# Expert pairs of a mixture-of-experts trunk: the selector transposes go ahead of the token gathering, in another PSUM bank, and ScalarE takes every second eviction

## Chip, cores and metric

One Trainium2 chip, one core. The metric is the device time of one execution in microseconds (us), median of several runs. Engines are named as in the profile: PE (TensorE matmul), PEld (its weight loads), DVE (VectorE), ACT (ScalarE), POOL (GpSimd), SP (SyncE, which issues nearly all transfers).

## The reference

Two layers over 256 tokens of width 1024. Each layer is an attention sublayer ("mixing") and a mixture of experts; the change touches the experts only. In float32:

```python
g_val, g_idx = lax.top_k(g_prob, 1)                  # one of 4 groups per token
e_val, e_loc = lax.top_k(e_prob, TOP_K)              # 2 of its 8 experts
gate = g_val * e_val / jnp.sum(e_val, axis=-1, keepdims=True)
...
def run_block(args):
    e, idx, g = args
    xb = xt[idx]
    hb = jax.nn.silu(xb @ w1[e]) * (xb @ w3[e])       # 1024 -> 512
    return (hb @ w2[e]) * g[:, None].astype(x.dtype)  # 512 -> 1024
...
y = jnp.zeros_like(xt).at[tok_buf].add(y_buf.reshape(-1, d))
```

There are 32 experts per layer, with three weight matrices of 2 MB each.

## The kernel before

**Slots and selectors.** Each expert has room for 64 tokens (C = 64). A selector matrix says which token goes to which place: `placed(q)` builds `Dm[q]` for four experts on VectorE, and `gated(i)` multiplies the part of pair i with the gate values into `Dg`. Experts run in pairs: pair i is experts 2i and 2i + 1, and there are n = 16 pairs.

**The loop over pairs** (L1410 to L1434) is unrolled, and PE takes its instructions in the order written there (a manual schedule for PE); the other engines' orders come from the framework's planner, and tiles of one name in a pool share one buffer. For pair i PE runs: `up(i, 0)`, the two up projections of the first expert (L1359, 16 matmuls, 32 records in the profile, into bank `ph`); `y_part(i - 1, 0)` and `y_part(i - 1, 1)`, the down projections of the pair before (L1384, into banks `py` and `px`); `glu(i, 0)`, four transposes into bank `T` (L1200), from which ScalarE (L1202) and VectorE (L1203, L1204) make `gT`; `up(i, 1)`; `combine(i - 1)` (L1395), which adds the pair before to the four accumulators `acc`; on odd i `gather(q)`, which picks the tokens of the next two pairs with 32 short matmuls (L1302) in four blocks of two column groups, banks `px`, `py`, `px`, `py`, each block evicted by two VectorE instructions to `xg` (L1308); `glu(i, 1)`, again into `T`; and `scatter(i + 1)`: two transposes of `Dg` (L1338), also into bank `T`, from which VectorE takes `DT` (L1341) and `gate` (L1342). Only then comes `up(i + 1, 0)`. On i = 3 a residual is added by eight matmuls (L1284).

**Start and end.** `start_up()` routes the tokens, runs `gather(0)`, the projections of pair 0, `scatter(0)` and `glu(0, 1)`. The last pairs (L1435 to L1445) and the two loops' surroundings are as they were.

**Weights** stream from HBM through a ring of slots: `ring.free(...)` after the last reader of a slot lets SP issue the next transfer of a fixed list. The list follows the order of use: the first expert of a pair, the down weights of the pair before, the second expert. Blocks of 1024 KB hold half a matrix (L241); the last experts' down weights come as 512 KB blocks (L275). After the last expert of layer 0 the list goes on with the attention weights of layer 1.

Of the kernel before, what the change touches and what calls it, by code (L numbers as in the profile page):

```python
# [9 lines left out]
F32 = mybir.dt.float32  # L10
I32 = mybir.dt.int32
AF = mybir.ActivationFunctionType
OP = mybir.AluOpType
# [5 lines left out]
C = 64  # L19
# [138 lines left out]
def program(tc, I, out):  # L158
    nc = tc.nc
# [7 lines left out]
    def pool_(**kw):  # L167
        return tc.tile_pool(reuse_waits="tile", **kw)
# [202 lines left out]
    def warm(ps, n):  # L371

        for _ in range(n):
            nc.tensor.matmul(ps, ones, ones, start=True, stop=True)
# [734 lines left out]
    def experts(l, lg, logits, late, c2, acc, routed, two_parts):  # L1109
        nonlocal h  # L1110
        p1 = c2.enter_context(pool_(name=f"moe{l}", bufs=1))
        wkp = c2.enter_context(pool_(name=f"wk{l}", bufs=1, space=PS, side="right"))

        def start_up():
# [5 lines left out]
            steps, pos, OH, pair, vals = routing(lg, p1, wkp)  # L1120
            Dm[0] = p1.tile([128, 2, 4 * C], F32R, name="Dm")
            gathers = gather(0)
            two = [steps(t) for t in range(2)]
            for ahead in two:
# [46 lines left out]
            glu(0, 0, hs)  # L1171
            ph = next(up)
            scatter(0, gated(0))
            glu(0, 1, evacuated(ph))

# [14 lines left out]
        def evacuated(hps):  # L1190

            hs = p1.tile([128, 4, 128], F32, name="hs")
            nc.scalar.activation(hs, hps.rearrange("q (p j) -> q j p", j=4), AF.Copy)  # L1193
            return hs
# [63 lines left out]
        st, Dm, xg, gTs = {}, {}, {}, {}  # L1258
# [29 lines left out]
        def placed(q, *ts):  # L1288

            n = len(ts)  # L1290
            at = slice(ts[0], ts[0] + n)
            pv = pos[:, at, 4 * q:4 * q + 4, None].to_broadcast([128, n, 4, C])
            nc.vector.tensor_tensor(Dm[q][:, at].rearrange("p t (e s) -> p t e s", e=4),
                                    io[:, None, None, :].to_broadcast([128, n, 4, C]), pv, op=OP.is_equal)

        def gather(q):

            xg[q] = flex.tile([128, 8, 4 * C], F32, name="xg", tag="H")

            def product(px, k, t):  # L1300
                for i, x in enumerate(two_parts):
                    nc.tensor.matmul(px[:, k % 2], x[:, t, k], Dm[q][:, t], start=k % 2 == t == i == 0,  # L1302
                                     stop=k % 2 == t == i == 1, skip_group_check=True)

            def out(px, k0):
                for k in range(k0, k0 + 2):
                    g, b = ln[:, k:k + 1], ln[:, 8 + k:9 + k]
                    st["last"] = nc.vector.tensor_scalar(xg[q][:, k], px[:, k - k0], g, b, op0=OP.mult, op1=OP.add)  # L1308

            if q == 0:  # L1310
                px = [wkp.tile([128, 2, 4 * C], F32, name=name) for name in ("px", "py")]
                for t in range(2):
                    for k in range(4):
                        product(px[k // 2], k, t)
                        if t and k % 2:
                            out(px[k // 2], k - 1)
                    yield
            for k0 in range(0 if q else 4, 8, 2):
                px = wkp.tile([128, 2, 4 * C], F32, name="py" if k0 % 4 else "px")
                for k in range(k0, k0 + 2):  # L1320
                    for t in range(2):
                        product(px, k, t)
                out(px, k0)
            yield

        def gated(i):

            Dg = p1.tile([128, 2, 2, C], F32, name="Dg")
            D4 = Dm[i // 2].bitcast(F32).rearrange("p t (e s) -> p t e s", e=4)[:, :, 2 * (i % 2):2 * (i % 2) + 2]
            gv = G[:, :, 2 * i:2 * i + 2, None].to_broadcast([128, 2, 2, C])  # L1330
            nc.vector.tensor_tensor(Dg, D4, gv, op=OP.mult)
            return Dg

        def scatter(i, Dg):

            pd = wkp.tile([128, 2, 128], F32, name="T")
            for t in range(2):
                nc.tensor.transpose(pd[:, t], Dg[:, t].rearrange("p e s -> p (e s)"), ident)  # L1338
            DT = p1.tile([128, 2, 128], F32R, name="DT", bufs=2)
            gate = p1.tile([128, 1], F32, name="gate", bufs=2)  # L1340
            nc.vector.tensor_scalar(DT, pd, 0.0, None, op0=OP.is_gt)  # L1341
            nc.vector.tensor_reduce(gate, pd.rearrange("p t s -> p (t s)"), axis=AX.X, op=OP.add)  # L1342
            st[i] = dict(DT=DT, gate=gate)
# [22 lines left out]
        def glu(i, e, hs):  # L1366
            gT = p1.tile([128, 4, C], F32, name=f"gT{e}", tag=("Dg", "Dm")[e] if i == n - 1 else f"gT{e}")
            act_pair(hs, gT)
            gTs[i, e] = gT

        def y_part(i, a, fill=None, bank=None):

            ys = [out_parts[:, j, a] for j in range(2)]
            st[i]["ys", a] = ys
            cols = i >= n - 2
            W = [[ring[(l, "w2", 2 * i + e, half)].rearrange("p (j d) -> p j d", j=4 if cols else 2) for half in range(2)]
                 for e in range(2)]
            py = wkp.tile([128, 512], F32, name=bank or ("px" if a else "py"))
            for j in range(4):
                if fill and j == 2:  # L1380
                    fill()
                for e in range(2):
                    w = W[e][a][:, j] if cols else W[e][j // 2][:, j % 2, 512 * a:512 * a + 512]
                    nc.tensor.matmul(py[C * e:C * e + C], gTs[i, e][:, j], w, start=j == 0, stop=j == 3)  # L1384
            gate = st[i]["gate"]
            nc.scalar.activation(ys[0], py, AF.Copy, scale=gate)  # L1386
            nc.vector.scalar_tensor_tensor(ys[1], py, gate, ys[0].bitcast(F32), op0=OP.mult, op1=OP.subtract)  # L1387
            if a:
                ring.free(*[(l, "w2", 2 * i + e, half) for half in range(2) for e in range(2)])

        def combine(i, *parts):

            for t, a in parts:
                for j, y in enumerate(st[i]["ys", a]):
                    nc.tensor.matmul(acc[t][a], st[i]["DT"][:, t], y, start=False, stop=i == n - 1 and j == 1,  # L1395
                                     skip_group_check=True)
                if i == n - 1:
                    nc.vector.bn_stats(sts[t][:, a], acc[t][a])
# [6 lines left out]
        def up(i, e):  # L1405
            *_, ph = up_proj(i, e)
            return evacuated(ph)

        with tc.manual_schedule(engines={mybir.EngineType.PE}):
            for i in range(n - 1):  # L1410
                if i:
                    hs = up(i, 0)
                    for a in range(2):
                        y_part(i - 1, a)
                    glu(i, 0, hs)
                    hs = up(i, 1)
                if i % 2:
                    q = (i + 1) // 2
                    Dm[q] = p1.tile([128, 2, 4 * C], F32R, name="Dm")
                    placed(q, 0, 1)  # L1420
                if i:
                    combine(i - 1, *every)
                if i == 2:
                    residual = residual_ffn()
                    next(residual)
                if i == 3:
                    next(residual)
                if i % 2:
                    for _ in gather(q):
                        pass  # L1430
                Dg = gated(i + 1)
                if i:
                    glu(i, 1, hs)
                scatter(i + 1, Dg)  # L1434
            hs = up(n - 1, 0)  # L1435
            *_, ph = up_proj(n - 1, 1, bank="py")
            glu(n - 1, 0, hs)
            hs = evacuated(ph)
            for i in (n - 2, n - 1):
                first, second = ("px", "py") if i == n - 2 else ("py", "px")  # L1440
                y_part(i, 0, bank=first)
                if i == n - 2:
                    glu(n - 1, 1, hs)
                y_part(i, 1, lambda: combine(i, (0, 0), (1, 0)), bank=second)
                combine(i, (0, 1), (1, 1))  # L1445
            if l < L - 1:
                warm(wkp.tile([128, 128], F32, name="py"), 16)
# [27 lines left out]
    for l in range(L):  # L1475
        experts(l, *mixing(l))
# [48 lines left out]
```

## Time and profile before

| | us |
|---|---|
| median of 3 runs | 1476.15 (1475.31 to 1477.61) |
| profiled execution, its own time | 1479.88 |
| span of its profile | 1478.2 |
| PE busy | 1377.2 (93%) |
| DVE busy | 617.6 (42%) |
| ACT busy | 408.7 (28%) |
| q1, SP's transfers, share of 16 DMA engines | 84.6% |

Times in rows are us from the start of the span; a mean of one instruction is in ns. Busy PE includes matmuls that wait inside the array, so its share is not a share of peak.

### The profile page before, as it was taken

How to read it: one execution, taken by the hardware profiler on the slowest of the kernel's cores; microseconds unless marked ns; L12 is line 12 of the kernel's file. 1: busy time of each engine (PE TensorE's matmuls, PEld its weight loads, DVE VectorE, ACT ScalarE, POOL GpSimd, SP SyncE). 2: the span in 40 equal slices, each digit the busy share in tenths (PEclk: the TensorE clock that was granted, in tenths of full speed). 3: DMA queues.
4: the chain of work that ended last, by engine and by line, in shares of the span. 5: the costliest groups of instructions: out<-in, count | busy, mean ns of one | idle time of the engine just before them, and what ended most of it. 6: DMA issues, size and time to landing. Idle time of an engine off the chain costs nothing. (4 is left out here: it accounts for less than half of the span.)

```text
span 1478.2 us, 20321 instructions
## 1 busy us (share of the span) xinstructions
PE 1377.2 (93%) x8018; PEld 844.1 (57%) x8020; DVE 617.6 (42%) x1491; ACT 408.7 (28%) x858; POOL 88.8 (6%) x71
## 2 busy tenths in 40 slices
PE   8999999799999999999989999997999999999996
PEld 8999998433434434434389999983434434434432
DVE  6767777522212212212167776875212212212214
ACT  5566454211111111111145664541111010111111
POOL 2000030130000000000020000301300000000001
PEclk9999999799999999999999999999999999999998
DMA  9633788599999999999973438887999999999994
GB/s 349 207 115 129 251 319 298 190 326 417 419 419 420 419 420 420 418 420 418 383 250 114 116 128 282 322 295 251 374 419 419 419 420 419 421 420 419 419 408 152
DMA packets 114836, 488.74 MB, mean 331 GB/s; under 512 B 8624, under 2 KB 20400, under 8 KB 75440
## 3 DMA queue, kind: packets, MB, share of 16 engines
q1 hardware_dynamic: 114016, 486.26, 84.6%
q8 instruction: 65, 1.06, 0.3%
q10 hardware_dynamic: 720, 1.12, 0.2%
q14 instruction: 35, 0.29, 0.1%
HBM read 486.30 MB, written 1.05 MB: 330 GB/s over the span
## 5 line engine op out<-in xcount | busy, mean ns | idle before, releaser
L1359 PE MATMUL ph<-wslot,xg 128*64 128x512 f32 x1920 | 427.4, 597 | 0.0
L1359 PEld LDWEIGHTS ph<-wslot,xg 128*64 128x64 f32 x1920 | 132.8, 137 | 249.8 <-issue 246.6
L473 DVE TENSOR_TENSOR split<-wslot,split 128x512 fp32r<-128x512 f32 (+1 forms) x272 | 191.4, 715 | 95.2 <-ACT split L472 62.2
L472 ACT ACTIVATE split<-wslot 128x512 fp32r<-128x512 f32 (+2 forms) x276 | 168.8, 616 | 139.9 <-PE mm L504 119.6
L502 PE MATMUL mm<-hThi,split 128*128 128x256 f32 x704 | 202.3, 287 | 0.0
L504 PE MATMUL mm<-hThi,split 128*128 128x256 f32 x704 | 197.6, 281 | 0.3
L503 PE MATMUL mm<-hTlo,split 128*128 128x256 f32 x704 | 196.7, 279 | 0.0
L1193 ACT ACTIVATE hs<-ph 128x512 f32<-128x512 f32 x60 | 35.9, 598 | 452.8 <-PE ph L1359 439.2
L1387 DVE SCALAR_TENSOR_TENSOR ys<-py,gate,ys 128x512 fp32r<-128x512 f32 x32 | 24.0, 751 | 294.2 <-ACT ys L1386 294.2
L502 PEld LDWEIGHTS mm<-hThi,split 128*128 128x128 f32 x704 | 132.5, 188 | 3.7 <-ACT split L472 1.3
L504 PEld LDWEIGHTS mm<-hThi,split 128*128 128x128 f32 x704 | 132.3, 188 | 1.6 <-DVE split L473 1.5
L503 PEld LDWEIGHTS mm<-hTlo,split 128*128 128x128 f32 x704 | 132.5, 188 | 0.5 <-issue 0.5
L1384 PE MATMUL py<-wslot,gT 128*64 128x512 f32 x512 | 115.9, 593 | 0.0
L1384 PE MATMUL px<-wslot,gT 128*64 128x512 f32 x512 | 115.8, 593 | 0.0
L1203 DVE SCALAR_TENSOR_TENSOR th<-th,T 128x256 f32<-128x256 f32 x64 | 26.6, 416 | 166.3 <-ACT th L1202 166.3
L1308 DVE TENSOR_SCALAR xg<-px,cp 128x256 f32<-128x256 f32 x64 | 31.9, 540 | 133.9 <-PE px L1302 133.9
L1384 PEld LDWEIGHTS px<-wslot,gT 128*64 128x64 f32 x512 | 36.4, 137 | 71.9 <-issue 71.2
L1384 PEld LDWEIGHTS py<-wslot,gT 128*64 128x64 f32 x512 | 36.3, 137 | 71.4 <-issue 68.6
L1395 PE MATMUL acc<-ys,DT 128*128 128x512 f32 x256 | 70.5, 412 | 4.3 <-ACT ys L1386 3.2
L1395 PEld LDWEIGHTS acc<-ys,DT 128*128 128x128 f32 x256 | 45.3, 188 | 43.2 <-issue 26.0
L1202 ACT ACTIVATE th<-T 128x256 f32<-128x256 f32 x64 | 24.6, 384 | 146.3 <-PE T L1200 146.1
L1387 DVE SCALAR_TENSOR_TENSOR ys<-px,gate,ys 128x512 fp32r<-128x512 f32 x32 | 24.0, 751 | 85.3 <-ACT ys L1386 85.3
(311 smaller groups left out, 1755.9 us busy)
## 6 DMA issues: line engine op xcount, KB each, us to landing
wslot<-in_expert_w_dram SPq DMA_DIRECT2D x304, 1024.0 KB, 19.9
wslot<-in_expert_w_dram SPq DMA_DIRECT2D x160, 512.0 KB, 8.6
wslot<-in_w_gate_dram SPq DMA_DIRECT2D x16, 2048.0 KB, 9.9
wslot<-in_w_in_dram SPq DMA_DIRECT2D x6, 2048.0 KB, 14.9
wslot<-in_w_branch_dram SPq DMA_DIRECT2D x8, 1024.0 KB, 6.3
wslot<-in_w_out_dram SPq DMA_DIRECT2D x4, 2048.0 KB, 16.3
wslot<-in_w_in_dram SPq DMA_DIRECT2D x4, 1024.0 KB, 14.7
wslot<-in_w_in_dram SPq DMA_DIRECT2D x4, 832.0 KB, 10.3
```

Of the source, the lines that this page charges most:

```text
L472: nc.scalar.activation(hi, w, AF.Copy)
L473: engine.tensor_tensor(lo, w, hi.bitcast(F32), op=OP.subtract)
L502: nc.tensor.matmul(ps, st[0], mv[0], start=start, stop=False)
L503: nc.tensor.matmul(ps, st[0], mv[1], start=False, stop=False)
L504: nc.tensor.matmul(ps, st[1], mv[0], start=False, stop=stop)
L1193: nc.scalar.activation(hs, hps.rearrange("q (p j) -> q j p", j=4), AF.Copy)
L1203: nc.vector.scalar_tensor_tensor(th, th, 1.0, ps[:, :, 0:C], op0=OP.add, op1=OP.mult)
L1308: st["last"] = nc.vector.tensor_scalar(xg[q][:, k], px[:, k - k0], g, b, op0=OP.mult, op1=OP.add)
L1359: nc.tensor.matmul(ph[C * s:C * s + C], x[:, k, c0:c0 + C], w[:, k % part], start=k == 0, stop=k == 7)
L1384: nc.tensor.matmul(py[C * e:C * e + C], gTs[i, e][:, j], w, start=j == 0, stop=j == 3)
L1387: nc.vector.scalar_tensor_tensor(ys[1], py, gate, ys[0].bitcast(F32), op0=OP.mult, op1=OP.subtract)
L1395: nc.tensor.matmul(acc[t][a], st[i]["DT"][:, t], y, start=False, stop=i == n - 1 and j == 1, skip_group_check=True)
```

## The change

The selector transposes of pair i + 1 are issued right after the combination of pair i - 1 and ahead of the gathering, instead of after `glu(i, 1)`; they go to bank `px` instead of `T` (but for pair 0). `gated(i + 1)`, which feeds them, is written ahead of the combination. In the gathering of q > 0 the blocks take the banks in the order `py`, `px`, `py`, `px`. In every gathering, that of the start too, the odd one of a block's two column groups is evicted by ScalarE (an Identity activation with scale and bias) instead of VectorE.

```diff
             def out(px, k0):
                 for k in range(k0, k0 + 2):
                     g, b = ln[:, k:k + 1], ln[:, 8 + k:9 + k]
-                    st["last"] = nc.vector.tensor_scalar(xg[q][:, k], px[:, k - k0], g, b, op0=OP.mult, op1=OP.add)
+                    if k % 2:
+                        nc.scalar.activation(xg[q][:, k], px[:, k - k0], AF.Identity, bias=b, scale=g)
+                    else:
+                        st["last"] = nc.vector.tensor_scalar(xg[q][:, k], px[:, k - k0], g, b, op0=OP.mult, op1=OP.add)
...
-                px = wkp.tile([128, 2, 4 * C], F32, name="py" if k0 % 4 else "px")
+                px = wkp.tile([128, 2, 4 * C], F32, name="px" if bool(k0 % 4) == bool(q) else "py")
...
-            pd = wkp.tile([128, 2, 128], F32, name="T")
+            pd = wkp.tile([128, 2, 128], F32, name="px" if i else "T")
...
                     placed(q, 0, 1)
+                Dg = gated(i + 1)
                 if i:
                     combine(i - 1, *every)
...
+                scatter(i + 1, Dg)
                 if i % 2:
                     for _ in gather(q):
                         pass
-                Dg = gated(i + 1)
                 if i:
                     glu(i, 1, hs)
-                scatter(i + 1, Dg)
```

## Rows read from the trace of the kernel before

**Rows 1.** The view of waits, whole span: total us, times, longest.
```profile
PE T L1338 <- DVE gT L1204: 46.1, 30, 1.5
```
**Rows 2.** Timeline of PE, layer 1: start, us, instruction, idle before.
```profile
1056.28 0.28 PE L1302 MATMUL px<-Dm,hi 128*128 128x256 f32 x1
...
1060.36 0.28 PE L1302 MATMUL py<-Dm,lo 128*128 128x256 f32 x1
1060.48 0.60 PE L1200 MATMUL T<-cp,hs 128*128 128x128 f32 x4
1062.62 0.41 PE L1338 MATMUL T<-cp,Dg 128*128 128x128 f32 x2 [1.54 <-DVE gT L1204]
1062.96 7.09 PE L1359 MATMUL ph<-wslot,xg 128*64 128x512 f32 x32
...
1086.42 0.60 PE L1200 MATMUL T<-cp,hs 128*128 128x128 f32 x4
1088.56 0.41 PE L1338 MATMUL T<-cp,Dg 128*128 128x128 f32 x2 [1.53 <-DVE gT L1204]
1088.89 7.09 PE L1359 MATMUL ph<-wslot,xg 128*64 128x512 f32 x32
```
**Rows 3.** The chain that ended last, two pairs of layer 1: start, us, what.
```profile
1148.45 7.02 PE ph L1359 x32
...
1204.52 7.02 PE ph L1359 x32
```
**Rows 4.** Timeline of VectorE around the gathering of pair 1, layer 1.
```profile
1057.43 1.00 DVE L1308 TENSOR_SCALAR xg<-px,cp 128x256 f32<-128x256 f32 x2 [8.33 <-PE px L1302]
...
1063.06 0.42 DVE L1341 TENSOR_SCALAR DT<-T 128x256 fp32r<-128x256 f32 x1 [0.59 <-PE T L1338]
...
1063.74 0.42 DVE L1331 TENSOR_TENSOR Dg<-Dm,G 128x256 f32<-128x256 f32 x1
```
**Rows 5.** Groups of ScalarE by line: busy us, mean ns, idle before and releaser.
```profile
L866 ACT ACTIVATE full<-tp,cp 128x256 f32<-128x256 f32 x8 | 4.3, 560 | 2.2 <-PE tp L368 2.2
```
**Rows 6.** Windows: length, engines' busy us, granted clock, DMA share, GB/s.
```profile
1056.00:1428.00 372.00, 349.84 (x1720) 149.63 (x1719) 85.65 (x181) 42.77 (x79) 3.71 (x3) 1.00 1.01 419
304.00:327.00 23.00, 23.00 (x102) 7.57 (x100) 3.34 (x7) 4.08 (x5) 9.03 (x6) 0.93 0.88 301
1034.00:1050.00 16.00, 16.00 (x78) 5.47 (x76) 2.26 (x5) 4.08 (x5) 4.96 (x3) 1.00 0.95 325
```
**Rows 7.** Each layer's last 1024 KB block: issue, landing, reader.
```profile
685.25 0.33 SPq L241 DMA_DIRECT2D wslot<-in_expert_w_dram  x1
...
1411.56 0.33 SPq L241 DMA_DIRECT2D wslot<-in_expert_w_dram  x1
...
wslot<-in_expert_w_dram SPq DMA_DIRECT2D x1, 1024.0 KB, 19.9
...
708.57 7.04 PE L1359 MATMUL py<-wslot,xg 128*64 128x512 f32 x32
...
1435.64 7.04 PE L1359 MATMUL py<-wslot,xg 128*64 128x512 f32 x32
```
**Rows 8.** Timelines of VectorE and PE, start of layer 1's experts.
```profile
1011.96 1.00 DVE L1308 TENSOR_SCALAR xg<-py,cp 128x256 f32<-128x256 f32 x2
...
1013.06 0.22 PE L1088 MATMUL T<-cnt,cp 32*32 32x1 f32 x2 [1.14 <-DVE neg L1054]
```
**Rows 9.** Layer 1's first attention weights: issue, landing, reader.
```profile
717.40 3.25 SPq L219 DMA_DIRECT2D wslot<-in_w_in_dram  x2
...
wslot<-in_w_in_dram SPq DMA_DIRECT2D x2, 832.0 KB, 12.2
...
736.72 2.46 ACT L472 ACTIVATE room<-wslot 128x832 fp32r<-128x832 f32 x3
```
**Rows 10.** After PE's pauses: a PE row of layer 0, a window of layer 1.
```profile
304.04 8.78 PE L1359 MATMUL ph<-wslot,xg 128*64 128x512 f32 x32
...
1030.00:1034.00 4.00, 2.15 (x12) 1.10 (x14) 3.11 (x8) 0.38 (x1) 0.00 (x0) 1.00 1.00 390
```

## The prediction

> **What bounds the kernel now.** I read the view of waits first, since the change takes a wait away: PE stood 30 times, 46.1 us in all, before the selector transposes until `gT` had left bank `T` [rows 1]. That is 15 times in each layer, once per pair. The timeline of PE shows two places: after an odd pair the transposes of `glu(i, 1)` start at 1060.48, and the selector follows only at 1062.62; after an even pair the same at 1086.42 and 1088.56. Then the next projections start at once [rows 2]. In the chain that ended last, nearly all else is PE without a pause, and two pairs take 1204.52 - 1148.45 = 56.1 us [rows 3]. So far PE sets the end, and 46 us of pauses look like 46 us to win.
>
> The windows speak against that. From 1056 to 1428 the 16 DMA engines were busy all the time (share 1.01) at 419 GB/s [rows 6]. Two pairs read 24 blocks of 1024 KB, 25.17 MB, which takes 60.1 us at that rate. PE eats them in 56.1. So the transfers are slower than PE already, and PE lives on a stock that was loaded before the loop and shrinks by 4 us every two pairs. Once it is gone, PE waits for weights, however short its own work.
>
> How much is left at the end is read from the last 1024 KB block of each layer (second half of `w3` of expert 31) [rows 7]. In layer 0 it was issued at 685.25 and landed 19.9 later, at 705.2. The 32 records that read these matrices start at 708.57; with 7.02 for 32 [rows 3], the 19th, the first to need this block, starts 3.9 later, at 712.5. It lay ready for 7.3 us. In layer 1: 1411.56 + 19.9 = 1431.5, needed at 1435.64 + 3.9 = 1439.5, 8.0 us. The sixteen smaller blocks behind it are needed later still, and I found none with less. No pause that the change removes comes after this place, so a layer's end can move by its stock and no further, unless the transfers move too.
>
> **The change part by part.** *Selector transposes ahead, other bank.* They need `Dg` and a free bank. VectorE makes `Dg` right after the gate of the pair before (1063.74) [rows 4], a pair ahead of its use, and `px` was emptied before the combination. So the wait goes: 1.54 of 46.1 / 30 per pair; the 0.34 of the two transposes only moves. Behind them `DT` and `gate` empty `px`, 0.68 from 1063.06 to 1063.74 [rows 4], while PE fills `py` with the first block of the gathering. One block is a quarter of 1056.28 to 1060.48 [rows 2], 1.05 with its gaps. Cover 1.05 against 0.68 and hand-overs: cost zero, and if that cover is gone, up to 0.7 on each of 14 odd pairs, 10 us of PE.
>
> *ScalarE's share of the evictions.* VectorE took 1.00 for the two of a block [rows 4]; ScalarE's nearest row, an activation of the same shape with scale and bias from `cp`, takes 0.56 [rows 5]. Side by side a block is free after 0.56; one after the other, after about 1.1. PE's gathering has 32 matmuls 0.12 apart, 3.8 us, in the 4.2 of [rows 2], so 0.4 of gaps can go in the first case and about 0.1 more comes in the second. No row shows both engines at one bank at the same time. I take the middle: nothing. Behind it `up(i + 1, 0)` now meets `xg` fresh, but it starts with the first column group and reads the last one some 6 us later, so that wait is covered.
>
> By the Trainium skill (PSUM — Partial Sum Buffer, "PSUM bank collisions raise a hardware error") two engines may not even read one bank at once, so the two evictions would have to take turns, and PE's own saving would be about 45 us instead of 52. By either the end comes out the same here, as the stock runs out first.
>
> PE's saving is thus 46 us, 23 in each layer, against stocks of 7.3 and 8.0.
>
> *What moves the transfers.* Before they are saturated, freed slots set them. The saving of pair 0 (1.5) frees slots earlier. In layer 0 the DMA engines were idle for (1 - 0.88) x 23 = 2.8 us between 304 and 327, so the stream can move by all 1.5; in layer 1 for (1 - 0.95) x 16 = 0.8 between 1034 and 1050, so by 0.8 [rows 6]. Bounds: 0 and 1.5 each.
>
> *The start.* The last two evictions of `gather(0)` take 1.00 on VectorE from 1011.96, and PE waits 1.14 for small VectorE work queued behind them until 1013.06 [rows 8]. With one of the two on ScalarE the queue is shorter by about 0.45, in both layers: everything behind, transfers too, starts that much earlier. Bounds 0 and 1.0 each.
>
> *Between the layers.* Layer 1's attention must start earlier by what layer 0 gains. Its first weights were issued from 717.40 on, two blocks over 3.25, with 12.2 to landing: the second lands near 731.3. ScalarE read them from 736.72, 2.46 for three instructions, the third at about 738.3 [rows 9]. After a shift of 9.3, with the transfers 2.0 earlier, that third one is wanted at 729.0 and there at 729.3. It just fits; PE needs the result over ten us later. I carry all of layer 0's gain, bounds all and nothing.
>
> **Sum.** Layer 0: 7.3 + 1.5 + 0.45 = 9.25. Layer 1: 8.0 + 0.8 + 0.45 = 9.25. Together 18.5; restarts after a wait for weights, for which I have no price, may eat some tenths, so 18. The profiled execution took 1479.88 (span 1478.2 and 1.7 around it), 3.7 (0.25%) above the median of the runs; 1479.9 - 18 = 1461.9 there, and 1476.15 - 18 = 1458 for the median.
>
> **Rivals.** *Part of it is lost* (1463 to 1469): layer 1's attention waits for its weights, or the transfers do not start earlier. For it: the fit above is within 0.3. Without layer 0's share 9.25 are left, 1466.9; without the earlier starts 15.3, 1460.8, which is still in the forecast.
>
> *The whole saving arrives*: 46 us, 1430. It would need 25.17 MB in 52.9 us, 476 GB/s. The saturated 372 us at 419 [rows 6] speak against it.
>
> *The change does not do what it says*: PE stands before the selector as long as before, now for `Dg` or `px`, because the planner puts `DT`, `gate` or `Dg` behind the evictions in VectorE's queue. Then 1476. To hide the gain, more than 15 of 23 us per layer would have to come back as new waits of 1 us per pair; the order in [rows 4] speaks against it, as does the stock, for which a third of the saving is enough.
>
> *Slower: the clock falls while PE waits for weights.* Where PE is starved it would stand about 23 + 23 - 18 = 28 us in short pauses that are not there now. After pauses of the start in layer 0 one projection took 8.78 instead of 7.09, with the granted clock at 0.93 over that window [rows 6, 10]: 1.7 more for (1 - 0.93) x 2 x 23 = 3.2 us at the lower of the two levels (1.2 instead of 2.4 GHz), half a microsecond per microsecond. In layer 1, with PE busy for 2.15 of 4 us, it stayed at 1.00 [rows 10]. A fall in mid-loop lets the stock grow back and costs nothing; one in the last pairs counts. It decides from 36 us at the low level there; the last two pairs of both layers at that level, 2 x 56 longer, would give 1458 + 112 = 1570, one last pair each (28 each) about 1514.
>
> [...]
>
> **How the numbers follow.** Forecast, own range 1454 to 1463: 0.60. Part lost, or a few us of low clock near an end: 0.18. Whole saving: 0.05. No change: 0.08. Slower: 0.09. The time is 1458. From 1453 to 1468 the forecast lies whole, with most of the part-lost case, together about 0.77 to 0.8; below it is the whole saving, above it the last two. Faster by over 0.2% (3 us, about what a measurement here can tell from none): 0.83; within: 0.08; slower: 0.09.
>
> **What would show it.** The wait of rows 1 gone; in odd pairs the projections at most 5.2 us after the combination instead of 1062.96 - 1056.28 = 6.7, where no weights are missing. New waits of PE for transfers of expert weights, some 14 us per layer, in the second half of each loop; windows there still at 419 GB/s; two pairs near 60 us instead of 56. The last 1024 KB block read as it lands, about 9 us earlier in layer 0 and 18 in layer 1. Granted clock 1.00 in both loops. Wrong would be: a block that lies ready for long while PE is starved for another reason, a wait of PE for `Dg`, `px` or `xg` of over 1 us per pair, a low clock near the ends, or layer 1's attention waiting for weights.

## The result, and the profile after

The changed kernel takes 1455.93 us (median of 4 runs, 1453.73 to 1457.2); the kernel before took 1475.73 beside it (1474.07 to 1477.61). The ratio is 0.9855, with a 95% interval of 0.9842 to 0.9868: 19 to 23 us faster, 1.5%; the two medians alone differ by 19.8. The forecast was 1458 with a range of 1453 to 1468. The profiled execution of the changed kernel took 1456.63 (span 1455.0), close to its median, while that of before lay 3.7 above its own; partly for that reason the two traces differ by 23.2 us.

The view of waits of the kernel after (total us, times, longest). PEld is PE's loading of weights:
```profile
PEld py L1387 <- DMA wslot<-in_expert_w_dram: 12.7, 16, 2.3
...
PEld py L1362 <- DMA wslot<-in_expert_w_dram: 8.1, 6, 2.3
...
PE py L1387 <- DMA wslot<-in_expert_w_dram: 6.2, 7, 1.4
...
PEld py L1302 <- ACT xg L1309: 5.4, 14, 1.3
...
PE py L1362 <- DMA wslot<-in_expert_w_dram: 4.2, 4, 1.4
```
The wait of [rows 1], 46.1 us before the selector, is gone. In its place PE waits for expert weights. Two lines of the same view of the kernel before, first for the evictions at the third block of the gathering, then the longest for expert weights:
```profile
PEld px L1302 <- DVE xg L1308: 4.8, 14, 0.3
...
PEld ph L1359 <- DMA wslot<-in_expert_w_dram: 3.1, 12, 0.3
```
Before, only weight loads waited for expert weights, 0.3 us at most at a time, and the multiplications never. The wait at the third block, the fourth line above, is an old one that grew from 4.8 to 5.4.

PE's timeline of the kernel after, the same two places of layer 1 as in [rows 2]: an odd pair, then an even one.
```profile
1038.86 2.14 PE L1398 MATMUL acc<-ys,DT 128*128 128x512 f32 x8
1040.84 0.38 PE L1341 MATMUL px<-cp,Dg 128*128 128x128 f32 x2
...
1045.64 0.60 PE L1200 MATMUL T<-cp,hs 128*128 128x128 f32 x4
1046.17 0.65 PE L1362 MATMUL ph<-wslot,xg 128*64 128x512 f32 x2
...
1069.64 0.38 PE L1341 MATMUL px<-cp,Dg 128*128 128x128 f32 x2
1069.85 0.60 PE L1200 MATMUL T<-cp,hs 128*128 128x128 f32 x4
1070.38 1.08 PE L1362 MATMUL ph<-wslot,xg 128*64 128x512 f32 x4
```
From the selector, which now follows the combination, to the next projections an odd pair takes 1046.17 - 1040.84 = 5.3 us, with the gathering in it (forecast: at most 5.2, before 6.7); an even pair 0.7. None of the rows shown has idle time ahead of it. While the stock lasts, two pairs take 53.0 us, by two rows of the chain that ended last (start, us, what):
```profile
1155.67 7.02 PE ph L1362 x32
...
1208.67 6.58 PE ph L1362 x29
```
In [rows 3] it was 56.1. PE really is 3 us faster per two pairs. Later that stops. PE's selectors of the kernel after, from the timeline:
```profile
1311.68 0.38 PE L1341 MATMUL px<-cp,Dg 128*128 128x128 f32 x2
...
1341.58 0.38 PE L1341 MATMUL px<-cp,Dg 128*128 128x128 f32 x2
...
1372.55 0.38 PE L1341 MATMUL px<-cp,Dg 128*128 128x128 f32 x2
...
1401.43 0.38 PE L1341 MATMUL px<-cp,Dg 128*128 128x128 f32 x2
```
Every second one: 60.9 and 59.9 us for two pairs, the 60.1 of the transfers. The chain, further on, says the same (start, us, what):
```profile
1232.89 3.45 PE ph L1362 x15
1236.34 19.89 DMA wslot<-in_expert_w_dram
...
1375.93 19.90 DMA wslot<-in_expert_w_dram
...
1395.89 19.94 DMA wslot<-in_expert_w_dram
...
1415.88 3.65 PE py L1362 x14
```
Before, the chain was PE nearly throughout. Now it leaves PE at 1236, runs through nine transfers end to end, and comes back to PE at 1415.88. The windows (length, engines' busy us, clock, DMA share, GB/s) beside [rows 6]:
```profile
330.00:720.00 390.00, 383.35 (x1825) 164.14 (x1825) 74.07 (x156) 60.11 (x112) 0.45 (x2) 1.00 1.02 417
1040.00:1410.00 370.00, 365.74 (x1759) 159.06 (x1757) 73.06 (x155) 58.37 (x108) 6.04 (x5) 1.00 1.01 419
304.00:327.00 23.00, 23.00 (x113) 9.43 (x110) 3.53 (x7) 4.67 (x6) 12.93 (x9) 1.00 0.98 359
1018.00:1034.00 16.00, 16.00 (x78) 5.36 (x75) 3.48 (x8) 2.44 (x5) 4.72 (x2) 1.00 1.02 377
```
The saturated rate is what it was, 417 and 419. What changed is the stretch ahead of it: 359 GB/s where there were 301, and 377 at a share of 1.02 where there were 325 at 0.95 (376 at 1.01 in the window that lies as far behind pair 0's selector as that of before). The last 1024 KB block of each layer, issue and first reader, beside [rows 7]:
```profile
680.53 0.33 SPq L241 DMA_DIRECT2D wslot<-in_expert_w_dram  x1
...
1395.89 0.33 SPq L241 DMA_DIRECT2D wslot<-in_expert_w_dram  x1
...
700.52 1.94 PE L1362 MATMUL py<-wslot,xg 128*64 128x512 f32 x8 [1.39 <-DMA wslot<-in_expert_w_dram]
...
1415.88 3.65 PE L1362 MATMUL py<-wslot,xg 128*64 128x512 f32 x14 [1.38 <-DMA wslot<-in_expert_w_dram]
```
With 19.9 to landing these blocks arrive at 700.4 and 1415.8 and are read at once. The 7.3 and 8.0 us for which they lay ready before are spent. They are read 12.0 and 23.6 us earlier than before, where I had 9 and 18; up to 3.7 of that is the profiled run of before, which was that far above its median.

### The profile page after: what moved, and what is told of

Same layout as the page of the kernel before. It is cut to its first block, busy times and chain, and to the rows that moved or that the text cites. A ratio compares the mean times of both kernels' runs of the same rounds, so it can differ in the third digit from the quotient of the medians.

```text
span 1455.0 us, 20334 instructions
## 1 busy us (share of the span) xinstructions
PE 1392.5 (96%) x8020; PEld 857.3 (59%) x8020; DVE 588.3 (40%) x1427; ACT 443.0 (30%) x922; POOL 89.9 (6%) x71
## 5 line engine op out<-in xcount | busy, mean ns | idle before, releaser
L1362 PEld LDWEIGHTS ph<-wslot,xg 128*64 128x64 f32 x1920 | 141.7, 137 | 244.5 <-issue 233.7
L1387 PE MATMUL py<-wslot,gT 128*64 128x512 f32 x512 | 125.5, 599 | 6.2 <-DMA wslot<-in_expert_w_dram 6.2
L1387 PE MATMUL px<-wslot,gT 128*64 128x512 f32 x512 | 121.8, 596 | 0.0
L1344 DVE TENSOR_SCALAR DT<-px 128x256 fp32r<-128x256 f32 x30 | 12.7, 425 | 224.0 <-PE px L1341 224.0
L1389 ACT ACTIVATE ys<-py,gate 128x512 fp32r<-128x512 f32 x32 | 22.0, 687 | 113.8 <-PE py L1387 113.8
L1389 ACT ACTIVATE ys<-px,gate 128x512 fp32r<-128x512 f32 x32 | 22.0, 687 | 89.0 <-PE px L1387 89.0
## 6 DMA issues: line engine op xcount, KB each, us to landing
wslot<-in_expert_w_dram SPq DMA_DIRECT2D x304, 1024.0 KB, 19.9
```

Source lines behind the costliest of these rows:

```text
L1362: nc.tensor.matmul(ph[C * s:C * s + C], x[:, k, c0:c0 + C], w[:, k % part], start=k == 0, stop=k == 7)
```

## The experiments

The theory: after the change the transfers set each layer's end. The gain is the stock of landed weights that PE may now spend, plus what the transfers start earlier, and PE time beyond that is worth nothing. Rivals: PE's work still sets the end, so that each microsecond counts in proportion; ScalarE's share brings part of it; the place in PE's order counts, not the bank.

**Fewer transfers, PE's work unchanged.** In the kernel after, for two or five experts of each layer, and in the kernel before for the same five. `SKIP` holds their numbers; `w3` of these experts is left out and `w1` is read in its place, so their results are others:
```
-            return two([((l, "w1", e), w1[l, e]), ((l, "w3", e), w3[l, e])])
+            if e in SKIP:
+                return two([((l, "w1", e), w1[l, e])])
...
-            keys = [[(l, w, 2 * i + e, j) for w in (("w1",) if fine else ("w1", "w3"))] for j in range(8 // part)]
+            keys = [[(l, w, 2 * i + e, j) for w in (("w1",) if fine or 2 * i + e in SKIP else ("w1", "w3"))] for j in range(8 // part)]
...
-                        w = ring[keys[k // 4][s]].rearrange("p (k f) -> p k f", k=4)
+                        w = ring[keys[k // 4][s % len(keys[0])]].rearrange("p (k f) -> p k f", k=4)
```


> The kernel after with fewer transfers: of experts 14 and 22 of each layer w3 is not loaded, and the blocks of w1 stand in for it, so those two experts' results are others; PE does the same work. A layer moves 4.2 MB less, 10 us at the 419 GB/s of the loop. If the transfers set the end, all of it shows until PE runs out of waits (some 16 us a layer): 1435 to 1438 us. If PE's work sets the end, 1454 to 1457 us.

> The kernel after, with w3 of experts 10, 14, 18, 22 and 26 of each layer not loaded and w1 in its place, so that their results are others; PE does the same work. A layer moves 10.5 MB less, 25 us at 419 GB/s. If the transfers set the end with PE's path some 12 to 16 us a layer behind them, the gain stops at PE's path: 1424 to 1432 us, near the 1430 us that the waits alone would give. If PE's work sets the end already, 1454 to 1457 us.

> The kernel before, with the same transfers left out (w3 of experts 10, 14, 18, 22 and 26 of each layer, w1 in its place, so that their results are others). PE waits for no transfer there, so if the kernel before was bound by PE, 25 us less of transfers a layer bring nothing: 1473 to 1477 us. If the transfers bound it too, 1440 us or less.


Measured: 1434.63, ratio to before 0.9709 (0.969 to 0.9727); 1428.57, 0.9666 (0.965 to 0.9682); and 1476.92, 0.9998 (0.9988 to 1.0007). Taking 20 us of transfers (at 419 GB/s) out of the changed kernel took 21 us off its time; taking out 50 took off only 27, and out of the kernel before, nothing. In the profile of the kernel after with five fewer, the line of the page on the chain that ended last, by engine:
```profile
PE 28%; DVE 2%; ACT 0%; issue 0%; DVEq 0%
```
and its PE selectors in the timeline:
```profile
1323.62 0.38 PE L1344 MATMUL px<-cp,Dg 128*128 128x128 f32 x2
...
1376.62 0.38 PE L1344 MATMUL px<-cp,Dg 128*128 128x128 f32 x2
```
No DMA is left in the chain, and two pairs take 53.0 to the end. That is PE's own path, 1428.6: the "whole saving" of the forecast's rival, which had 1430. The transfers keep 27 of the 48 us that the kernel could have won.

**More work for PE**, in both kernels:
```
                 if i:
                     combine(i - 1, *every)
+                for _ in range(3):
+                    nc.tensor.matmul(acc[0][0], zeros, zeros[:, 0:1].to_broadcast([128, 512]), start=False, stop=False,
+                                     skip_group_check=True)
```


> The kernel after with more work on PE: three matmuls of zeros (128x512, bf16) onto the sums behind the combination of each of the 15 turns of the loop, in both layers; they add zero. One of these took 0.38 us by its record where it stands alone, less behind another, so that the added work is 22 to 34 us in all. If the transfers set the end, it fits into PE's waits of some 16 us a layer: 1456 to 1460 us. If PE's work sets it, 1478 us or more.

> The kernel before with the same added work on PE: three matmuls of zeros in each of the 15 turns of the loop, in both layers. PE waits for no transfer there, and the stock of landed weights that is left at a layer's end is 7 to 8 us. If the theory is right, the kernel before was bound by PE and all of the added work shows: 1498 us or more. If the kernel before was already bound by its transfers, under 1485 us.


Measured: 1460.12, 0.989 (0.9875 to 0.9905) in the kernel after; 1502.58, 1.017 (1.0156 to 1.0184) in that of before. So the same work costs 26 us before and 4 to 5 after. Even the 4 to 5 are mostly something else. The view of waits, first the kernel after with the load, then that of before with it:
```profile
PE py L1362 <- PEq L1209: 8.8, 2, 4.8
```
```profile
PE py L1359 <- PEq L1209: 9.1, 2, 4.9
```
Behind the test for overflowing tokens PE waits for its own sequencer once in each layer. Without the load the two came to 4.5 in the kernel after (4.0 in layer 0 and 0.4 in layer 1), and to 5.5 before. With it the one in layer 1 is long too, 4.3 us more, ahead of the loop. Nothing seems to cover it: from the issue of layer 0's last 1024 KB block to pair 0's selector of layer 1 it is 342.0 us with the load, and 334.7 to 337.6 in the kernel after and in four runs without the load (VectorE alone, bank alone, pair 1 old, late pairs old). What remains for 45 matmuls a layer is about 1 us in the kernel after; in that of before, where the two waits grew by 3.6, it is 22.

**Where a wait stands.** The kernel after, with the old bank for pair 1 alone, and for the pairs from 8 on:
```
-            pd = wkp.tile([128, 2, 128], F32, name="px" if i else "T")
+            pd = wkp.tile([128, 2, 128], F32, name="px" if i > 1 else "T")
```
```
-            pd = wkp.tile([128, 2, 128], F32, name="px" if i else "T")
+            pd = wkp.tile([128, 2, 128], F32, name="px" if 0 < i < 8 else "T")
```


> The kernel after, but the selector of pair 1 goes into T as before, in each layer; 14 of 15 selectors a layer stay in px. It gives back 2 waits of 1.5 us of the 30 that went (3 of 46 us). If the start of the transfers sets the end, these two are worth all they delay: 1.5 us, and 1.7 us where PE's clock falls again for the projections behind it, in each layer, so 1459 to 1462 us. If PE's work in the loops sets the end and 46 us of it brought 20, two of 30 waits bring 1.3 us: 1457 us.

> The kernel after, but the selectors of pairs 8 to 15 go into T as before, in each layer: 16 of the 30 waits of 1.5 us come back, 24 us of PE's time. In the changed kernel PE waits some 16 us for expert weights in the second half of each layer. If the transfers set the end, the 12 us a layer fit into these waits: 1456 to 1459 us. If PE's work sets the end, 16 of 30 waits give back more than half of the gain: 1466 us or more.


Measured: 1459.98, 0.9884 (0.9869 to 0.9899) with pair 1 old; 1455.13, 0.9855 (0.984 to 0.987) with the late pairs old, the ratio of the kernel after to the digit. The views of waits, pair 1 old and late pairs old:
```profile
PE T L1341 <- DVE gT L1204: 3.1, 2, 1.5
```
```profile
PE T L1200 <- DVE gate L1345: 9.4, 10, 0.9
...
PE py L1302 <- ACT xg L1309: 4.6, 10, 1.1
```
Two waits of 1.5 us at the head of the loops cost 4 us; in that trace PE's clock also fell behind one of them (below). The late ones cost nothing. They were a smaller load than I had put down: with the selector ahead, the old bank costs a wait of 0.9 at the next transposes, not 1.5, and the two lines above are 7.5 and 3.5 us more than in the kernel after, 11 instead of 24. Of the two runs the first is the stronger evidence against PE's work in proportion, which would have had 1457; the extra load above does what the second was meant to do.

**One part of the change alone.** First the kernel after with VectorE evicting all:
```
-                    if k % 2:
-                        nc.scalar.activation(xg[q][:, k], px[:, k - k0], AF.Identity, bias=b, scale=g)
-                    else:
-                        st["last"] = nc.vector.tensor_scalar(xg[q][:, k], px[:, k - k0], g, b, op0=OP.mult, op1=OP.add)
+                    st["last"] = nc.vector.tensor_scalar(xg[q][:, k], px[:, k - k0], g, b, op0=OP.mult, op1=OP.add)
```
Then the kernel before with ScalarE's share alone, which is the same edit the other way round, and the kernel before with the bank alone, the selector at its old place:
```
-            pd = wkp.tile([128, 2, 128], F32, name="T")
+            pd = wkp.tile([128, 2, 128], F32, name="px" if i else "T")
```


> The kernel after, but VectorE evicts every block of the gathered tokens, as in the kernel before; the selector stays ahead of the gathering in px. If the transfers set the end of a layer and the gain comes from the selector alone, this run takes 1456 to 1458 us: the pair of evictions took 1.00 us on VectorE alone and takes 0.53 and 0.56 us in turn in the changed kernel, so ScalarE's share saves nothing in the loop, and at most the start of layer 1 (some 1.6 us) is lost. If the share brings part of the gain, it is 1462 us or more.

> The kernel before with one edit of the change alone: ScalarE evicts every second block. If the selector brings the gain, 1472 to 1475 us, that is no more than the earlier start of layer 1. If the share brings it, 1465 us or less.

> The kernel before with one edit alone: the selector goes into px instead of T, but stays behind the gathering and the transposes of the gate, and VectorE evicts all. If the wait of 1.5 us a pair was for the bank T, it is gone here too and the time is 1457 to 1460 us. If the place in PE's order matters, because the selector there waits for VectorE's evictions of px or for Dg, the wait stays under another name and the time is 1470 us or more.


Measured: VectorE alone 1456.54, 0.9866 (0.9848 to 0.9884), which can't be told from the kernel after. ScalarE's share alone 1478.65, 1.0017 (1.0006 to 1.0028): a little slower than before, where I expected a little faster. The bank alone 1459.34, 0.988 (0.9863 to 0.9898): nearly all of the gain. So the bank alone is enough; on top of it the place in PE's order and ScalarE's share add no more than a few tenths of a per cent between them. Whether the place alone would be enough was not run. The late pairs above had the new place and the old bank, and 16 selectors brought back 11 us of waits, 0.7 each instead of 1.5, so the place may well be worth much by itself. ScalarE's share alone has these waits of PE:
```profile
PE T L1341 <- DVE gT L1204: 46.4, 30, 1.8
...
PE px L1302 <- ACT xg L1309: 4.1, 14, 0.3
```
The second line was 0.2 us in the kernel before, but there the weight loads already waited at the same place, the 4.8 above; with the share they wait 7.4, two of the 16 times in the first gathering. The new waits are thus nearer to the difference, 2.6 us, than to 3.9. In that kernel PE set the end, so they show, as 2.5 us. Why the evictions are no faster on two engines is seen in the timelines of VectorE and ScalarE in the kernel after, at pair 1's gathering in layer 1:
```profile
1042.31 0.53 DVE L1311 TENSOR_SCALAR xg<-py,cp 128x256 f32<-128x256 f32 x1
1043.39 0.54 DVE L1311 TENSOR_SCALAR xg<-px,cp 128x256 f32<-128x256 f32 x1 [0.54 <-PE px L1302]
...
1042.88 0.56 ACT L1309 ACTIVATE xg<-py,cp 128x256 f32<-128x256 f32 x1 [3.30 <-DVE xg L1311]
1043.96 0.57 ACT L1309 ACTIVATE xg<-px,cp 128x256 f32<-128x256 f32 x1 [0.52 <-DVE xg L1311]
```
ScalarE starts when VectorE has finished with the same bank: 0.53 and 0.56 in turn, 1.13 for a block that VectorE took 1.00 for alone [rows 4]. In the kernel after with VectorE alone, the weight loads wait 3.5 us at the third block instead of 5.4.

**Pair 0's selector ahead too**, on top of the kernel after:
```
             glu(0, 0, hs)
-            ph = next(up)
             scatter(0, gated(0))
+            ph = next(up)
...
-            pd = wkp.tile([128, 2, 128], F32, name="px" if i else "T")
+            pd = wkp.tile([128, 2, 128], F32, name="px")
```


> The kernel after, with pair 0's selector handled like the others: in px, and ahead of the second half of the second expert's projections. In the changed kernel PE still waits 0.9 us there for VectorE's reduction, once in each layer, before the expert transfers run without a gap. If the start of the transfers sets the end of each layer, the wait is worth 0.9 us a layer: 1454 us, 1.5 to 2 us under the kernel after. If PE's work in the loop set the end, it would be the same 2 us, so this run does not tell these two apart; it asks whether a version under both is to be had. With no gain, neither holds at the start of a layer.


Measured: 1454.69, 0.9863 (0.9846 to 0.988). The two waits of 0.9 us are gone from its trace, but its time can't be told from that of the kernel after. Whether it beats it is open.

## Why the prediction was right, point by point

**What bounds the kernel, before and after.** Shown. Before, PE set the end: fewer transfers brought nothing and more work all of its price. After, the transfers do: the reverse on both. The step from "46 us of pauses" to "7 to 8 us of stock per layer" was the one that made the forecast, and both stocks were spent to 0.1 us.

**The wait goes.** Right, and the other bank is enough for it: with the bank alone the time was 1459.34. `DT` and `gate` were covered as reckoned. The wait at the gathering's third block, 5.4 us in 14 places on PE's weight loads, was there before with 4.8 and is for the evictions.

**ScalarE's share: nothing.** I took the middle between side by side and in turn. The trace shows in turn, the dear end, and on a PE-bound kernel a loss of 2.5 us. In the kernel after it is hidden behind the transfers. The Trainium skill (PSUM — Partial Sum Buffer, "PSUM bank collisions raise a hardware error") lets no two engines read one bank at once, so that the program must have them take turns. The trace agrees: ScalarE starts at 1042.88, behind 1042.31 + 0.53. But what makes it wait here is a semaphore of the program, so no run put the bank itself to the test.

**Transfers that start earlier.** The mis-sized term. It had 1.5 us in layer 0 and 0.8 in layer 1 for the first turn's selector. Take the time from pair 0's selector on PE to the issue of the last 1024 KB block, which is a layer's stretch of transfers. For the kernel before with ScalarE's share alone, from the timelines of PE and SP:
```profile
297.95 0.44 PE L1341 MATMUL T<-cp,Dg 128*128 128x128 f32 x2
...
681.81 0.33 SPq L241 DMA_DIRECT2D wslot<-in_expert_w_dram  x1
...
1025.97 0.44 PE L1341 MATMUL T<-cp,Dg 128*128 128x128 f32 x2
...
1409.94 0.33 SPq L241 DMA_DIRECT2D wslot<-in_expert_w_dram  x1
```
and PE's two rows for the kernel after, whose issues stand above:
```profile
299.69 0.44 PE L1341 MATMUL T<-cp,Dg 128*128 128x128 f32 x2
...
1015.22 0.44 PE L1341 MATMUL T<-cp,Dg 128*128 128x128 f32 x2
```
The same from the other traces, us in layer 0 and layer 1:

| pair 1's selector waits as before | | it doesn't | |
|---|---|---|---|
| before | 385.1, 382.6 | after | 380.8, 380.7 |
| ScalarE's share alone | 383.9, 384.0 | VectorE alone | 381.3, 380.2 |
| before with the load | 384.8, 384.7 | bank alone | 381.0, 381.5 |
| after, pair 1 old | 382.9, 384.4 | after, late pairs old | 380.6, 380.0 |
| | | after with the load | 380.8, 380.0 |

The means are 384.0 and 380.7: 3.4 us per layer, not 1.5 and 0.8. (With pair 0's selector ahead the row from which this counts has moved, so that run is left out.) My cap from the idle share of the DMA engines, 0.8 us in layer 1, was wrong, and so was the wait itself as the upper bound.

Part of the excess is PE's clock, which the sum left out. Windows at pair 1's first projections, with columns as in [rows 6]: layer 0 of the kernel before, layer 1 with pair 1 old, layer 0 of the kernel after:
```profile
304.00:308.00 4.00, 4.00 (x14) 1.24 (x14) 1.09 (x3) 0.00 (x0) 0.00 (x0) 0.58 0.80 321
```
```profile
1018.00:1022.00 4.00, 3.17 (x10) 1.02 (x11) 1.74 (x5) 0.00 (x0) 0.00 (x0) 0.61 0.99 366
```
```profile
304.00:308.00 4.00, 4.00 (x22) 1.38 (x20) 0.00 (x0) 0.00 (x0) 0.00 (x0) 1.00 1.01 355
```
After the waits of 0.9 and 1.5 us ahead of pair 1's projections the granted clock fell in five of the eight stretches on the left of the table, to 0.94 over the 28 us from pair 0's selector. In the other three, and in all ten on the right, it stayed at 1.00. The five with the fall (385.1, 384.0, 384.8, 384.7, 384.4) have a mean of 384.6, the three without (382.6, 383.9, 382.9) one of 383.1. By these few stretches the wait without a fall is worth 2.4 us of transfers and the fall 1.5 more, near the 1.7 that the projection of [rows 10] lost. The forecast had seen that fall, but priced it in a rival and not in this term, though it stands behind the very wait that goes. Why a wait of 1.5 us is worth 2.4 even without it stays open.

With 3.4 in place, the sum is 7.3 + 8.0 + 3.4 + 3.4 = 22.1, within the measured 19 to 23.

**The start.** The 0.45 a layer from ScalarE's share is not shown: the share alone was slower, and leaving it out of the kernel after cost 0.11%, less than the intervals. The term was 0.9 of the 18.

**Pauses and the clock.** PE's pauses are as long in all as I reckoned, 27 us by the run with five fewer against 28. The clock fell once in the loops. Windows of the kernel after, around that place:
```profile
1352.00:1356.00 4.00, 2.07 (x8) 0.31 (x5) 0.00 (x0) 0.00 (x0) 0.00 (x0) 1.00 1.02 424
1356.00:1360.00 4.00, 4.00 (x12) 1.26 (x14) 0.00 (x0) 0.67 (x1) 0.00 (x0) 0.57 1.01 418
```
PE was busy for 2.07 of 4 us, and then ran at a granted clock of 0.57 over the next window, most of it at the lower of the two levels (1.2 of 2.4 GHz), while the transfers went on at 418. Sixty microseconds later the last block is read as it lands, so the fall cost nothing, as a fall in mid-loop should. The rival's case, a low clock in the last pairs, didn't come. The Trainium skill (TensorE: Matmul & The Clock Gate, "HAM oscillation — how this bites in real kernels") describes a kernel whose waits for DMA, longer than any here, throw the clock back each time. Here the longest was 2.3 us, and one fall came with the 22 waits of the first two lines of waits above, so no run has the page's case. The 8.78 us projection of [rows 10], by which I priced it, was no fixture of the kernel before either: with ScalarE's share alone the same projection took 7.09 in layer 0, and the fall came in layer 1.

**Between the layers** all of layer 0's gain was carried: from the first matmul that reads layer 0's last block to pair 0's selector of layer 1 it was 1015.22 - 700.52 = 314.7 us after; before, with the block needed at 712.5, 1028.94 - 712.5 = 316.4. What the forecast called a fit was none by its own numbers, since ScalarE's third instruction would have found its weights 0.3 us late. It came out well because these transfers were issued 4.7 us earlier than before (712.72 for 717.40), as the last block was, and not 2.0.

## What to carry to other kernels

Before pricing a wait on an engine, compare what a loop turn needs from the transfers with what it needs from the engine; if the transfers are slower, the stock left at the last block, not the sum of the waits, is what can be won. To see which of the two sets the end, take transfers away and leave the work, and add work and leave the transfers. Here a wait ahead of the saturated stretch cost more than its length, in part because PE's clock fell behind it, and waits inside the stretch cost next to nothing.

## What was not expected of the hardware

PE's wait for its own sequencer behind the branch of L1209 was 0.4 us in layer 1 of the kernels before and after, and 4.8 to 4.9 in both kernels with 45 more matmuls a layer: more work in the loop made a stall of 4.4 us ahead of it, and why is not shown. Two engines that shared a bank's evictions took 1.13 us for what one took 1.00 for.
